# Rotating 96 images by 180 degrees on one core: one load queue in place of two, the third group loaded in two parts, and the order of the turning work

## The chip, the core and the metric

The kernel runs on one core of one Trainium2 chip. The metric is the device time of one execution in microseconds (us). Before the change its median is 121.94 us over three runs, which lie between 121.81 and 122.52 us.

## The reference

```python
def setup_inputs():
    batch, c, h, w = 32, 3, 256, 256
    return {"x": np.random.randn(batch, c, h, w).astype(np.float32)}

def reference(x):
    return np.rot90(x, k=2, axes=(-2, -1)).astype(np.float32)
```

There are 32 x 3 = 96 images of 256 x 256 float32. A turn by 180 degrees reverses both axes, so each image, seen as one run of 65,536 numbers, is written backwards. Nothing is computed; 25.17 MB are read and 25.17 MB are written.

## The kernel before, in words

Each image is cut into four quarters of E = 16384 numbers (64 KB). The 384 quarters make three groups of 128, and each group fills one tile in the on-chip memory SBUF: A, Bt and Ct, with one quarter in each of the 128 partitions. A fourth tile T has J = 2048 columns and is the scratch of the swaps. The quarters of A and Bt are taken alternately from the first 256 quarters, and Ct holds the last 128.

The reversal is done in two steps. Inside a quarter, `swap` (lines 56 to 60) exchanges `w` columns at the left with `w` columns at the right, both reversed, with three VectorE copies through T; line 47 is the copy itself, and it keeps the copies in the order in which they are written. `turn` (line 69) does this from column `lo` to column `hi` of the left half in steps of at most J, so a full turn of a tile is four swaps, or twelve copies of 128x2048. The order of the four quarters of an image is reversed by the store's addresses (line 53, the `::-1`).

Two queues issue transfers: SyncE's (called SPq in the profile, hardware queue q1) and ScalarE's (ACTq, hardware queue q10). Both feed the same 16 DMA engines. SyncE issues the load of A (line 64), then the load of Ct (line 67), and all stores. ScalarE issues the load of Bt (line 66); a memset of 256 columns of Bt on VectorE (line 65) stands ahead of it, so that ScalarE's load waits for it. Each load is one transfer of 128 rows of 64 KB.

The order written out by hand is: turn A except its innermost 2048 columns on either side of the middle; store the first LEAD = 256 columns of A (line 77), a small transfer of 128 pieces of 1 KB; turn Bt up to MID = 2560; turn the rest of A and store the remaining 16128 columns of A (line 80); turn the rest of Bt and store Bt (line 82); turn Ct and store Ct (line 84). A DMA instruction on SyncE holds up the ones written behind it until its own waits are over. A store reads its tile only when the copies that wrote the stored columns are done.

Of the kernel before, what the change touches and what calls it, by code (L numbers as in the profile page):

```python
# [2 lines left out]

os.environ.setdefault("NEURON_RT_ULTRASERVER_MODE", "4")

# [4 lines left out]


@with_exitstack
def kernel(
    ctx: ExitStack,
    tc: tile.TileContext,
    x: bass.AP,
    out: bass.AP,
):
    nc = tc.nc  # L20
    P = 128

    B, C, H, W = x.shape
    L = H * W
    G = 32
    E = L // 4
    J = E // 8

    xr = x.rearrange("b c h w -> (b c) (h w)").rearrange(
        "m (s e) -> (m s) e", s=4)  # L30
    om = out.rearrange("b c h w -> (b c) (h w)").rearrange(
        "m (s e) -> m s e", s=4)
    rows = 2 * P
    x4 = [xr[0:rows:2], xr[1:rows:2], xr[rows:rows + P]]
    o4 = [om[0:2 * G, 1::2], om[0:2 * G, 0::2], om[2 * G:3 * G]]

    pool = ctx.enter_context(tc.tile_pool(name="slots", bufs=1))
    A = pool.tile([P, E], x.dtype, tag="A")
    Bt = pool.tile([P, E], x.dtype, tag="B")
    Ct = pool.tile([P, E], x.dtype, tag="C")  # L40
    T = pool.tile([P, J], x.dtype, tag="T")

    def back(t, lo, hi):
        return t[:, hi - 1:(lo - 1 if lo else None):-1]

    def copy(dst, src):
        tc.keep_in_program_order(nc.vector.tensor_copy(out=dst, in_=src))  # L47

    def load(t, g, lo, hi, queue=nc.sync):
        return queue.dma_start(out=t[:, lo:hi], in_=x4[g][:, lo:hi])  # L50

    def store(t, g, lo, hi):
        return nc.sync.dma_start(
            out=o4[g][:, ::-1, lo:hi], in_=t[:, lo:hi])

    def swap(t, lo, w):
        hi = E - lo - w
        copy(T[:, 0:w], back(t, hi, hi + w))
        copy(t[:, hi:hi + w], back(t, lo, lo + w))
        copy(t[:, lo:lo + w], T[:, 0:w])  # L60

    MID = 2560
    LEAD = 256
    load(A, 0, 0, E)
    nc.vector.memset(Bt[:, 0:256], 0.0)  # L65
    load(Bt, 1, 0, E, nc.scalar)
    load(Ct, 2, 0, E)

    def turn(t, lo, hi):
        while lo < hi:  # L70
            w = min(J, hi - lo)
            swap(t, lo, w)
            lo += w

    half = E // 2
    turn(A, 0, half - J)
    store(A, 0, 0, LEAD)
    turn(Bt, 0, MID)
    turn(A, half - J, half)
    store(A, 0, LEAD, E)  # L80
    turn(Bt, MID, half)
    store(Bt, 1, 0, E)
    turn(Ct, 0, half)
    store(Ct, 2, 0, E)


# [1 line left out]
_INS = ['x']  # L88
_OUTS = [((32, 3, 256, 256), 'float32')]


# [23 lines left out]
```

## Time and profile before

| what | value |
|---|---|
| median of three runs | 121.94 us (121.81 to 122.52) |
| the profiled execution's own time | 121.9 us |
| its span, from first to last instruction | 120.1 us |
| VectorE busy | 44.9 us, 40 instructions |
| bytes by DMA | 50.33 MB, mean 419 GB/s over the span |
| DMA packets' time, share of 16 engines' span | q1 81.3%, q10 16.1% |
| first packet starts, last packet ends (packet records) | 1.74 us, 118.99 us |

A span begins with the core's first instruction; the remaining 1.8 us of the device time lie around it. Times inside the span are counted from its start. In a row of the timeline, the first number is when an instruction starts and the second how long it takes. A DMA issue is short on its queue; its landing is told as the time from the issue until the transfer's completion signal, and that time contains whatever the DMA engines still had to do ahead of it. The trace also records every packet that a DMA engine moved, with its size, start and duration; a load of 128 rows has 128 packets of 65,536 bytes.

### The profile page before, as it was taken

Reading aid. Unit: us, or ns where it says so; the run is one execution under the profiler, and the core shown is the slowest. Engines: PE = TensorE matmul, PEld = TensorE weight load, DVE = VectorE, ACT = ScalarE, POOL = GpSimd, SP = SyncE. Lnnn points to the kernel's source line nnn. Section 1 sums busy time; section 2 is a strip of 40 time slices with the busy share of each in tenths; the row PEclk is TensorE's granted clock in tenths of the full one; section 3 lists DMA queues with packets and bytes.
Section 4 is the critical chain, followed back from the end, with each engine's and each line's share of the span. In section 5 each row is a group of like instructions: output and inputs, shape, how many; then the busy total and the mean of one; then the engine's idle time right before and its main releaser. Section 6 shows DMA issues by size and latency. Waiting matters only on the chain.

```text
span 120.1 us, 97 instructions
## 1 busy us (share of the span) xinstructions
DVE 44.9 (37%) x40; POOL 0.2 (0%) x4
## 2 busy tenths in 40 slices
DVE  0000000000000899999999999999400000000000
POOL 0000000000000000000000000000000000000000
DMA  9888988898889988998899777988898889888980
GB/s 349 349 349 371 677 349 349 349 698 349 349 349 633 415 349 349 546 502 349 349 387 687 344 344 344 687 349 349 349 698 349 349 349 698 349 349 349 677 371 0
DMA packets 1008, 50.33 MB, mean 419 GB/s; under 512 B 112, under 2 KB 240, under 8 KB 240
## 3 DMA queue, kind: packets, MB, share of 16 engines
q1 hardware_dynamic: 864, 41.94, 81.3%
q10 hardware_dynamic: 144, 8.39, 16.1%
HBM read 25.17 MB, written 25.17 MB: 419 GB/s over the span
## 4 chain that ended last, share of the span: by engine, by line
DVE 38%; DMA 32%; issue 1%
DMA A<-in_x_dram 32%; DVE T L47 13%; DVE Bt L47 9%; DVE A L47 8%; DVE Ct L47 8%
## 5 line engine op out<-in xcount | busy, mean ns | idle before, releaser
L47 DVE COPY T<-A 128x2048 f32<-128x2048 f32 x4 | 4.9, 1226 | 38.4 <-DMA A<-in_x_dram 38.3
L47 DVE COPY T<-Bt 128x2048 f32<-128x2048 f32 (+2 forms) x5 | 5.1, 1014 | 0.2
L47 DVE COPY Bt<-T 128x2048 f32<-128x2048 f32 (+2 forms) x5 | 5.1, 1014 | 0.2
L47 DVE COPY Bt<-Bt 128x2048 f32<-128x2048 f32 (+2 forms) x5 | 5.1, 1013 | 0.2
L47 DVE COPY T<-Ct 128x2048 f32<-128x2048 f32 x4 | 4.9, 1227 | 0.1
L47 DVE COPY Ct<-T 128x2048 f32<-128x2048 f32 x4 | 4.9, 1227 | 0.1
L47 DVE COPY A<-T 128x2048 f32<-128x2048 f32 x4 | 4.9, 1227 | 0.1
L47 DVE COPY A<-A 128x2048 f32<-128x2048 f32 x4 | 4.9, 1227 | 0.1
L47 DVE COPY Ct<-Ct 128x2048 f32<-128x2048 f32 x4 | 4.9, 1226 | 0.1
L65 DVE MEMSET Bt<- 128x256 f32 x1 | 0.3, 272 | 0.9 <-PEq L99 0.9
L99 POOL MEMSET const-bfloat16-1.0<- 128x1 bf16 x1 | 0.1, 102 | 0.0
L99 POOL MEMSET const-uint8-127<- 128x1 uint8 x1 | 0.1, 102 | 0.0
L99 POOL MEMSET const-float32-0.0<- 128x1 f32 x1 | 0.1, 99 | 0.2 <-issue 0.2
L99 POOL MEMSET const-float32-1.0<- 128x1 f32 x1 | 0.1, 99 | 0.0
## 6 DMA issues: line engine op xcount, KB each, us to landing
out_dram<-A SPq DMA_DIRECT2D x1, 8064.0 KB, 20.9
out_dram<-A SPq DMA_DIRECT2D x1, 128.0 KB, 18.4
A<-in_x_dram SPq DMA_DIRECT2D x1, 38.7
Bt<-in_x_dram ACTq DMA_DIRECT2D x1, 43.1
Ct<-in_x_dram SPq DMA_DIRECT2D x1, 60.1
out_dram<-Bt SPq DMA_DIRECT2D x1, 29.6
out_dram<-Ct SPq DMA_DIRECT2D x1, 33.9
```

The lines of the kernel that those rows point to most:

```text
L47: tc.keep_in_program_order(nc.vector.tensor_copy(out=dst, in_=src))
L65: nc.vector.memset(Bt[:, 0:256], 0.0)
L99: nc = _bacc.Bacc("TRN2", target_bir_lowering=False, num_devices=1)
```

## The change

All four loads are now issued by SyncE, one behind the other: A, then Bt, then Ct as two transfers, rows 0 to 111 and rows 112 to 127. The memset goes, and ScalarE issues nothing. The pieces of the turning work change: A is turned except its innermost KEY = 128 columns on either side of the middle; the first 256 columns of A are stored as before; Bt is turned up to half - LATE = 6144 columns in place of 2560; then a new copy of 112 partitions by 8 columns from Ct into T stands in the order, which reads rows that the first of the two Ct transfers writes, and whose result nothing uses; then the 128 key columns of A are turned, and A's second store is issued. The rest of Bt (2048 columns), its store, the turn of Ct and its store follow as before. In the changed kernel the lines of `swap` and of the helpers are the same, and the two Ct loads are lines 68 and 69.

```diff
-    MID = 2560
+    R = P - 16
     LEAD = 256
+    LATE = 2048
+    KEY = 128
     load(A, 0, 0, E)
-    nc.vector.memset(Bt[:, 0:256], 0.0)
-    load(Bt, 1, 0, E, nc.scalar)
-    load(Ct, 2, 0, E)
+    load(Bt, 1, 0, E)
+    nc.sync.dma_start(out=Ct[0:R, :], in_=x4[2][0:R, :])
+    nc.sync.dma_start(out=Ct[R:P, :], in_=x4[2][R:P, :])
...
-    turn(A, 0, half - J)
+    turn(A, 0, half - KEY)
     store(A, 0, 0, LEAD)
-    turn(Bt, 0, MID)
-    turn(A, half - J, half)
+    turn(Bt, 0, half - LATE)
+    copy(T[0:R, 0:8], back(Ct, 0, 8)[0:R])
+    turn(A, half - KEY, half)
     store(A, 0, LEAD, E)
-    turn(Bt, MID, half)
+    turn(Bt, half - LATE, half)
     store(Bt, 1, 0, E)
     turn(Ct, 0, half)
     store(Ct, 2, 0, E)
```

## The prediction

> **What bounds the kernel now.** I read the DMA parts of the page first, because the kernel only moves data.
>
> ```profile
> DMA  9888988898889988998899777988898889888980
> DMA packets 1008, 50.33 MB, mean 419 GB/s; under 512 B 112, under 2 KB 240, under 8 KB 240
> ...
> q1 hardware_dynamic: 864, 41.94, 81.3%
> q10 hardware_dynamic: 144, 8.39, 16.1%
> ```
>
> The 16 DMA engines are busy in every slice but the last. The two shares add to 97.4%. 50.33 MB over 16 engines are 48 rows of 64 KB for each, so one row costs at most 0.974 x 120.1 / 48 = 2.44 us. The packet records agree: after the first row of each engine, all 352 load rows up to 59 us took 2.418 to 2.429 us, and the store rows of Bt and Ct 2.418 to 2.441. So a core's floor here is 48 x 2.42 = 116.2 us, and the packets run from 1.74 to 118.99 us, 117.2 us. About 1 us is not floor: the first rows are slow (median 3.11 us, 0.69 over), and some engines idle up to 0.4 us between loads and stores.
>
> The chain looks different, and has to be read with the issues beside it:
>
> ```profile
> DVE 38%; DMA 32%; issue 1%
> ...
> out_dram<-A SPq DMA_DIRECT2D x1, 8064.0 KB, 20.9
> out_dram<-A SPq DMA_DIRECT2D x1, 128.0 KB, 18.4
> A<-in_x_dram SPq DMA_DIRECT2D x1, 38.7
> Bt<-in_x_dram ACTq DMA_DIRECT2D x1, 43.1
> Ct<-in_x_dram SPq DMA_DIRECT2D x1, 60.1
> out_dram<-Bt SPq DMA_DIRECT2D x1, 29.6
> out_dram<-Ct SPq DMA_DIRECT2D x1, 33.9
> ```
>
> It walks back from the last store through VectorE, but that store was issued at 85.4 us and took 33.9 us to land, although 8 rows per engine need 19.4: it queued behind two others for 14 us. VectorE is early there and does not bound. Now the place where the order does matter, the change from loads to stores:
>
> ```profile
> 58.51 1.23 DVE L47 COPY A<-T 128x2048 f32<-128x2048 f32 x1
> 59.76 0.55 SPq L53 DMA_DIRECT2D out_dram<-A  x1
> ...
> 70.31 0.54 SPq L53 DMA_DIRECT2D out_dram<-Bt  x1
> ```
>
> A's large store is issued at 59.76 and its first packets start at 60.97 to 61.20; the engines end their last load rows at 60.32 to 60.85 and fill the gap with the 1 KB pieces. The later stores are issued 10 us and more before their turn.
>
> **The change, part by part.**
>
> *One queue in place of two.* SyncE issues four loads in a row; an issue took 0.38 to 0.43 us, so the last leaves at about 2.4 us, 39 us before an engine needs it. What goes is the sharing of rows between q1 and q10. A then lands after 8 rows: 1.95 (mean first start) + 0.69 + 8 x 2.42 = 22.0 in place of 39.45, Bt at 41.4 in place of 44.3. The DMA engines do the same rows at the same 2.42 us, so this is worth nothing by itself. Its bounds: 0.69 us of gain, if the slow first rows come from the second queue's issue, and 0.3 us of loss. I take 0.
>
> *VectorE.* The memset (0.27) goes. Copies of 512, 1536 and 2048 columns took 427, 960 and 1227 ns, about 160 ns plus 0.52 ns a column; so the recut swaps cost 3 x 1.23 in place of 3 x (0.43 + 0.96) for Bt, and 3 x (1.16 + 0.23) in place of 3 x 1.23 for A: +0.48 - 0.48. The 8-column copy costs 0.16. All lies under the transfers: A is turned by 22.0 + 12 x 1.25 = 37.0, Bt's first three swaps run from 41.4 to 52.8, and then VectorE waits.
>
> *The added wait.* The copy from Ct waits for all 112 rows. Behind it on VectorE stand A's key swap, the rest of Bt and Ct; behind those on SyncE A's large store, then all others. The store is ready 0.18 + 3 x 0.25 = 0.93 us after the 112 rows, and its packets come 1.2 us after that, 2.1 us in all. If the last 16 rows took one row's time, 2.42 us, that and the 1 KB pieces (0.4 us) just cover it: 0 to +0.3 us. If the 16 rows take longer it is hidden wholly. Bt's store would be issued 3 x 1.25 = 3.8 us after A's, needed 19 us after it; Ct's 15 us after the last 16 rows land, needed 39 us after. Nothing there.
>
> *The third group as 112 rows and 16.* This decides. In the trace every transfer touches all 128 partitions, eight rows for each engine, and the rows keep their 2.42 us to 0.5% whatever the other engines do; so the limit is a private path of 64 KB in 2.42 us, 27.1 GB/s, for each share of eight rows, 16 paths in all. The trace does not say whether that path sits in the DMA engine or at the partitions it writes. Sixteen neighbouring rows are the case that separates them. Lower bound: each engine takes one row on a path of its own, 2.42 us. Upper bound: the 16 rows are two shares of eight, on two paths, 8 x 2.42 = 19.4 us. Between lie depths of two (4.84) and four (9.68). I take four: the nearest row is the store of Ct, whose output address is made of 32 runs of four neighbouring partitions, and it goes out at full speed, so runs of four can be the unit dealt to a path; 16 neighbours are then four runs on four paths. So this transfer costs 9.68 in place of the 2.42 that those rows had in the whole load: +7.26. For the 112 rows the depth is seven if the engines are the limit (16.9 us), eight wherever a path keeps all its eight rows (19.4 us): 0 to +2.42. An engine that is through with its seven starts on its sixteenth early, so the two excesses partly overlap: +7.26 to +9.68 together. I take the middle, +8.5.
>
> [...]
>
> **The sum.** Before: loads end at 41.4 + 19.4 = 60.8 (recorded: 60.85), and stores and completion take the rest. After: 60.8 + 8.5 = 69.3, then the same 24 store rows, since each engine keeps its own rows and the slowest sets the end. Span 120.1 + 8.5 = 128.6; device 121.9 + 8.5 = 130.4. The profiled 121.9 is the median of the three runs, so nothing is to be corrected.
>
> **The rivals.** A difference of about 1% (1.2 us) is what this measurement tells from no change.
>
> *The limit sits in the DMA engines (not slower).* Place: lines 68 and 69. Each engine moves seven rows and then one, each 2.42 us, 8 x 2.42 as before, and the loads end at 60.8. Then A's store decides: 112 rows in at 58.5, its packets at 60.6 to 60.9. It decides as soon as the depth of the 16 rows is one. Time 121.6 to 122.4. For it: one constant duration for loads and stores, whose addresses are cut differently (64 x 2 for A and Bt, 32 x 4 for Ct). Against: all of these span 128 partitions, and a deal without collisions would look the same.
>
> *A shallow collision.* Depth two, 4.84 us, or a depth of four half hidden under the 112 rows: +2 to +6, 124 to 128 us.
>
> *A deep collision.* The upper bound, two paths: +16.9 + 2.4, 141 us. Or the 112 rows themselves are dealt row by row, so that at each of seven steps the engines write 16 neighbours: 7 x 9.68 = 67.7 in place of 16.9, and with the last 16 about 180 us. Against the latter: engines drift apart by up to 1 us already in the first rows (1.74 to 2.72), which loosens a lockstep.
>
> *Faster.* All of the 0.69 us of the first rows and the idle 0.4 us together give 120.8, still within 1%; below that only rows under 2.418 us would help, and no load row is.
>
> **How the numbers follow.** The forecast, depth four, +6 to +10.5 us with the uncertain overlap, has its own range of 127.9 to 132.4 and a chance of 0.55. Shallow: 0.10. Limit in the engines: 0.26. Deep: 0.07. Faster by over 1%: 0.02. So slower by over 1% 0.72, within 1% 0.26. The range has to reach to the engines' case, whose lower end with a little gain at the first rows is 121.4; it goes up to 132.4 and leaves out the deep cases and the faster one, 0.09.
>
> **What would show it.** Right: the rows of Ct's last transfer take about 9.7 us each, the two Ct transfers land about 29 us after Bt in place of 19, A's store packets begin at 69 to 70 us, and the store rows are unchanged. The rows of the 112 transfer should vary, some at 4.8 us. If they are all 2.42 while the 16 rows are slow, the sum is 7.3 and the time 129.2. Wrong: all Ct rows at 2.42 us, and the loads over at 61; or idle DMA engines between 60 and 64 us, which would make the wait on the 112 rows the cause.

## The result and the profile after

The changed kernel takes 142.44 us (median of six runs, 142.31 to 142.92) against 121.98 us before (six runs, 121.81 to 122.52): a ratio of 1.168, 95% interval 1.167 to 1.170. It is 20.5 us slower; the forecast was +8.5 us in a range up to 132.4.

From the page of the changed kernel, the DMA lines of the 40 slices (tenths of busy time, then GB/s) and the queue:

```profile
DMA  8696969799798599999390699999999999999990
GB/s 298 298 597 298 597 298 578 317 466 429 317 578 187 112 298 298 298 298 224 75 299 0 230 432 459 422 459 423 410 410 466 429 448 429 448 410 429 466 392 0
DMA packets 1024, 50.33 MB, mean 358 GB/s; under 512 B 128, under 2 KB 256, under 8 KB 256
...
q1 hardware_dynamic: 1024, 50.33, 97.0%
```

The DMA engines are as busy as before (97.0% of a longer span, 97.4% before), but the mean rate fell from 419 to 358 GB/s. Busy is the time that packets take, not the bytes that they move. From the thirteenth slice to the twenty-third (a slice is 3.5 us) the rate is low. Cut by stages, the columns being the stretch, VectorE's and GpSimd's busy time, the clock, the DMA share and GB/s:

```profile
2.00:41.00 39.00, 14.52 (x12) 0.00 (x0) 1.00 0.96 415
41.00:71.00 30.00, 11.04 (x9) 0.00 (x0) 1.00 1.11 258
71.00:82.00 11.00, 4.55 (x8) 0.00 (x0) 1.00 0.77 177
82.00:140.00 58.00, 14.71 (x12) 0.00 (x0) 1.00 0.95 411
```

A packet is counted in the stretch in which it starts, so a share can pass 1. Before the change, the last 20 us of the loads had this rate:

```profile
41.00:61.00 20.00, 19.41 (x18) 0.00 (x0) 1.00 1.03 444
```

The loads of A and Bt (to 41 us) and the stores (from 82 us) run at full rate, 415 and 411 GB/s. Between them lie the two transfers of the third group, at 258 and 177 GB/s. The packet records show it row by row. They do not name the engine; below, the rows are sorted by their start and taken 16 at a time, one for each engine. All sizes are 64 KB.

```
rows of Ct, changed kernel     took, ns (least / median / most)
first of seven                 4076 / 4291 / 4555
second                         4780 / 4791 / 4876
third                          4647 / 4663 / 4853
fourth                         2861 / 3106 / 4888
fifth                          3405 / 3572 / 4702
sixth                          4204 / 4509 / 4652
seventh                        4606 / 4708 / 5304
the last 16 rows               7847 / 8334 / 8842
every row of A and Bt but the first   2418 to 2427
```

VectorE and the added wait, from the timeline:

```profile
52.29 1.23 DVE L47 COPY Bt<-T 128x2048 f32<-128x2048 f32 x1
74.76 0.17 DVE L47 COPY T<-Ct 112x8 f32<-112x8 f32 x1 [21.25 <-DMA Ct<-in_x_dram]
74.97 0.23 DVE L47 COPY T<-A 128x128 f32<-128x128 f32 x1
...
75.74 0.55 SPq L53 DMA_DIRECT2D out_dram<-A  x1
```

The copy waits 21.25 us for the 112 rows, and A's large store is issued at 75.74 in place of 59.76. That looks like the cause, and the chain supports it at first sight, because it walks back from the last store through VectorE to a load:

```profile
DMA 29%; DVE 22%; another core or an unknown queue 17%; issue 1%; SPq 0%; DVEq 0%
...
out_dram<-A SPq DMA_DIRECT2D x1, 8064.0 KB, 25.4
out_dram<-A SPq DMA_DIRECT2D x1, 128.0 KB, 55.8
Ct<-in_x_dram SPq DMA_DIRECT2D x2, 76.4
A<-in_x_dram SPq DMA_DIRECT2D x1, 21.8
Bt<-in_x_dram SPq DMA_DIRECT2D x1, 40.9
```

But the last load row ends only at 81.25, after that issue, so the store was in the queue in good time. The difference of the spans, 140.5 - 120.1 = 20.4 us, is the difference of the times at which the last load row ends: 81.25 against 60.85. It has three terms: the 112 rows took 30.0 us on the mean engine where 7 x 2.42 = 16.9 were free of trouble (+13.1), the 16 rows 8.34 in place of 2.42 (+5.9), and the slowest engine ended 1.63 us behind the mean in place of 0.23 (+1.4).

### The profile page after: what moved, and what is told of

It reads as the page before. It is cut to its first block, busy times and chain, and to the rows that moved or that the text cites. A ratio compares the mean times of both kernels' runs of the same rounds, so it can differ in the third digit from the quotient of the medians.

```text
span 140.5 us, 99 instructions
## 1 busy us (share of the span) xinstructions
DVE 44.8 (32%) x40; POOL 0.2 (0%) x4
## 2 busy tenths in 40 slices
DMA packets 1024, 50.33 MB, mean 358 GB/s; under 512 B 128, under 2 KB 256, under 8 KB 256
## 3 DMA queue, kind: packets, MB, share of 16 engines
q1 hardware_dynamic: 1024, 50.33, 97.0%
## 4 chain that ended last, share of the span: by engine, by line
DMA 29%; DVE 22%; another core or an unknown queue 17%; issue 1%; SPq 0%; DVEq 0%
DMA Bt<-in_x_dram 29%; DVE T L47 7%; DVE Ct L47 7%; DVE Bt L47 7%; DVE A L47 0%; SPq L50 0%; DVEq L47 0%
## 5 line engine op out<-in xcount | busy, mean ns | idle before, releaser
L47 DVE COPY T<-Ct 128x2048 f32<-128x2048 f32 (+1 forms) x5 | 5.1, 1016 | 23.8 <-DMA Ct<-in_x_dram 23.7
L47 DVE COPY T<-A 128x2048 f32<-128x2048 f32 (+2 forms) x5 | 5.1, 1013 | 22.7 <-DMA A<-in_x_dram 22.6
L47 DVE COPY T<-Bt 128x2048 f32<-128x2048 f32 x4 | 4.9, 1227 | 4.8 <-DMA Bt<-in_x_dram 4.7
L47 DVE COPY A<-A 128x2048 f32<-128x2048 f32 (+2 forms) x5 | 5.1, 1014 | 0.2
L47 DVE COPY A<-T 128x2048 f32<-128x2048 f32 (+2 forms) x5 | 5.1, 1014 | 0.2
L47 DVE COPY Bt<-T 128x2048 f32<-128x2048 f32 x4 | 4.9, 1227 | 0.1
L47 DVE COPY Bt<-Bt 128x2048 f32<-128x2048 f32 x4 | 4.9, 1226 | 0.1
```

## The experiments

The theory after the result, an estimate from rows of 4.1 to 5.3 and 7.8 to 8.8 us where 2.42 was usual: a row goes at 2.42 us only if its engine is alone on the path to the partition it writes; several partitions share a path; and the transfers of 112 and 16 rows make engines meet there. The rivals: the wait, the one queue, the mere number of transfers, or a limit inside the engines.

**Whole group, wait kept.**

```diff
-    nc.sync.dma_start(out=Ct[0:R, :], in_=x4[2][0:R, :])
-    nc.sync.dma_start(out=Ct[R:P, :], in_=x4[2][R:P, :])
+    load(Ct, 2, 0, E)
```

> The changed kernel with the third group loaded as one transfer of 128 rows; the copy from Ct then waits for all of it. Theory of colliding rows (the part loads write some partitions over a path that two or four engines share): all rows at 2.42 us, loads over at 61 us; the wait for the whole group costs the 2.1 us from landing to the first packets of A's large store, less the 0.4 us of 1 KB pieces: 123.4 to 124.0 us. Rival, that the one queue or the wait itself costs the 20 us: 140 to 142.4 us.

124.68 us, ratio 1.023 (1.020 to 1.026). Of the 20.5 us 2.7 are left, although the one queue, the order of turning and the copy from Ct stay. Its timeline:

```profile
61.66 0.17 DVE L47 COPY T<-Ct 112x8 f32<-112x8 f32 x1 [8.07 <-DMA Ct<-in_x_dram]
...
62.64 0.55 SPq L53 DMA_DIRECT2D out_dram<-A  x1
```

Here the wait is uncovered: the last load row ends at 61.28 (60.85 before), A's large store is issued at 62.64, its first packets come at 63.84 (60.97 before). These 2.9 us are the difference of the profiled spans, 123.0 against 120.1, so the wait accounts for the 2.7 us of the medians. They are 0.7 more than the upper end expected: the copy starts only 0.38 us after the last load row has ended, and the loads end 0.4 us later than before.

**Only the split, in the kernel before.** The edit is the change's two transfers in place of line 67, and nothing else.

> The kernel before, with nothing changed but the third group's load, which becomes the two transfers of 112 and 16 rows. Colliding rows: the 20 us come back, 140 to 143 us, with rows of 4 to 5 us in the first part and of about 8 us in the second; a little less if the rows of Bt, taken in turn from the other queue, loosen the collisions. Rival (one queue, or the wait): 121.5 to 122.5 us.

142.47 us, ratio 1.167 (1.165 to 1.169): the whole loss, with two queues and without the copy. A's large store is issued as early as before the change (59.76):

```profile
59.81 0.54 SPq L53 DMA_DIRECT2D out_dram<-A  x1
```

The slow rows have the changed kernel's pattern: 4.1 to 4.9 us in five of the seven steps (three rows of the last took 5.0 to 5.9), mostly 2.7 to 3.8 in the fourth and fifth, and 7.2 to 8.8 for the last 16 rows.

**The same bytes split by columns.**

```diff
+    CUT = E - J
+    load(Ct, 2, 0, CUT)
+    load(Ct, 2, CUT, E)
```

in place of the two row transfers.

> The changed kernel with the third group split by columns, 14336 and then 2048 of all 128 partitions, in place of by rows. The bytes ahead of the signal are the same seven eighths, the number of transfers and the wait are the same. Colliding rows: nothing collides, loads over at 61 us, A's large store comes as the loads end: 121.6 to 122.4 us. Rival, that any second transfer for the group or the wait costs: 130 us or more.

122.15 us, ratio 1.002 (1.001 to 1.003). Two transfers and a signal after seven eighths of the bytes, both on all 128 partitions, cost 0.15 us here. A's store packets begin at 61.15, 0.2 us after the loads' end at 60.95:

```profile
58.97 0.17 DVE L47 COPY T<-Ct 112x8 f32<-112x8 f32 x1 [5.62 <-DMA Ct<-in_x_dram]
...
59.95 0.55 SPq L53 DMA_DIRECT2D out_dram<-A  x1
```

**Without the copy from Ct.** Line 81 of the changed kernel goes; the row split stays.

> The changed kernel without the 112x8 copy, so that A's key columns are turned and A's large store is issued at about 54 us, 22 us earlier; the row split stays. Colliding rows: the store still queues behind the slow rows, 142.0 to 142.5 us, as with the wait. Rival, that the wait costs: the 20 us shrink by most of the 22 us.

142.89 us, ratio 1.171 (1.169 to 1.173). A's large store is issued 21 us earlier, and nothing is gained:

```profile
54.40 0.55 SPq L53 DMA_DIRECT2D out_dram<-A  x1
```

These four settle that the split by rows is the cause, and that the 21 us of waiting on VectorE were its effect.

**The ground for the next runs: the store early.** The third group is whole, the copy is gone, and `turn(A, half - KEY, half)` and A's large store stand right behind the first store. Bt is then turned in one go.

> All loads from SyncE, the third group whole, no copy from Ct, and A's large store issued as soon as A is turned (about 38 us), so that it queues behind the loads. This is the ground for the runs that split the third group otherwise. Colliding rows: rows at 2.42 us throughout and no idle engine between loads and stores, 121.4 to 122.2 us. Rival, that an early store disturbs the loads: 123 us or more.

122.81 us, ratio 1.006 (1.004 to 1.008), above the first expectation and just under the rival's. The loads' last row of each engine took 3.3 to 3.8 us; more on this at the end. On this ground the third group's load is cut in other ways.

**112 rows as seven transfers of every seventh partition.**

```diff
-    load(Ct, 2, 0, E)
+    for r in range(7):
+        nc.sync.dma_start(out=Ct[r:112:7, :], in_=x4[2][r:112:7, :])
+    nc.sync.dma_start(out=Ct[112:P, :], in_=x4[2][112:P, :])
```

> As the run with the early store, but the 112 rows come as seven transfers of 16 rows, every seventh partition (0, 7, 14 ... 105, then 1, 8 ... and so on), and rows 112 to 127 as an eighth. If the transfer of 112 rows gives each DMA engine seven neighbouring rows, this is the same sequence of partitions at the engines: rows of 3 to 4.9 us in the same pattern, 29 to 31 us for the seven, 141.5 to 143.5 us in all. If the transfer of 112 rows is dealt out otherwise, or a transfer of 112 rows is slow for its count, the time is another: 132 us or less, or over 150.

142.5 us in one run. The medians of the seven steps are 4.35, 4.73, 4.79, 2.90, 3.56, 4.63 and 4.71 us, against 4.29, 4.79, 4.66, 3.11, 3.57, 4.51 and 4.71 for the transfer of 112 rows. The medians differ by at most 0.21 us; the reading is that the one transfer gives each engine seven neighbouring rows, and that at each step the engines write partitions seven apart. The fourth step shows what may be a single collision: two engines took 4.73 and 4.74 (4.86 and 4.89 in the changed kernel), about twice 2.42, and the others 2.7 to 3.2. In the fifth, two took 4.24 and 4.43 and the others 3.6 to 3.7.

**Sixteen rows at a time, two ways.** The same eight transfers of 16 rows, to every eighth partition or to neighbours:

```diff
+    for r in range(8):                    # every eighth partition
+        nc.sync.dma_start(out=Ct[r:P:8, :], in_=x4[2][r:P:8, :])
```
```diff
+    for r in range(0, P, 16):             # neighbours
+        nc.sync.dma_start(out=Ct[r:r + 16, :], in_=x4[2][r:r + 16, :])
```

> The third group as eight transfers of 16 rows, each to every eighth partition. [...] If a path serves eight neighbouring partitions, or if the limit is in the DMA engines, no two rows meet: 122 us.

> The third group as eight transfers of 16 rows, each to 16 neighbouring partitions; the same number and size of transfers as with every eighth partition. Paths of four neighbours: four rows meet on each of four paths, 9.68 us a row, 77.4 us for the group in place of 19.4, 180 us in all. Paths of eight neighbours: 19.4 us a row, 155 us, 257 us in all. Limit in the DMA engines, or a cost for each transfer alone: the same time as with every eighth partition.

One run each: 143.63 and 176.98 us. From the stages of the run with every eighth partition, then of the run with neighbours:

```profile
41.00:82.00 41.00, 14.72 (x12) 0.00 (x0) 1.00 1.01 211
82.00:140.00 58.00, 14.72 (x12) 0.00 (x0) 1.00 0.99 429
```
```profile
41.00:116.00 75.00, 14.72 (x12) 0.00 (x0) 1.00 1.01 125
116.00:174.00 58.00, 14.72 (x12) 0.00 (x0) 1.00 0.96 416
```

The load stage has 211 and 125 GB/s with full DMA engines (share 1.01), and the stores behind it full rate again (429 and 416). The rows took 5.11 us (median of 128) and 9.22 us: 2.1 and 3.8 times 2.42. The bytes and the number of transfers are the same; what differs is which rows, and so which partitions, go together. So the limit is not in the engines. The reading, an estimate from the factors 2.1 and 3.8, is that two engines meet on a path with every eighth partition, and four with 16 neighbours. By it a path of eight neighbouring partitions is ruled out, as it would have left every eighth partition free of collisions.

One rival stands untested: row and partition go together in all these loads, so the rows that are read at one time lie differently in DRAM too, and no run moves the one without the other. That the partitions decide is the author's estimate and was not shown.

The run with every eighth partition says one thing more. Its sequence is what a load of 128 rows would be if it gave each engine eight neighbouring rows. Whole loads take 2.42 us a row and not 5.11, so by this reading they are dealt to the engines in another way than the 112 rows; how, no trace here shows.

**Two halves of 64 rows.** `range(0, P, 64)` with transfers of 64 neighbouring rows.

> As the run with the early store, but the third group comes as two transfers of 64 neighbouring rows. [...] If two large transfers of equal size are free of collisions: 123 us.

143.0 us in one run, against the 123 us expected of two transfers free of collisions; the rows took 5.12 us (median; 5.11 with every eighth partition), and the group about 40 us. Two large equal parts are no better.

**A store in two parts.** All loads are whole; A's large store goes out as 48 images' rows (96 partitions) and 16 (32 partitions).

```diff
-    store(A, 0, LEAD, E)
+    for m in (slice(0, 48), slice(48, 64)):
+        nc.sync.dma_start(out=o4[0][m, ::-1, LEAD:E],
+                          in_=A[2 * m.start:2 * m.stop, LEAD:E])
```

> As the run with the early store, all loads whole, but A's large store goes out as two transfers, of 96 partitions and of 32. [...] If only writes into the partitions collide: 122.5 to 123.2 us.

141.39 us in one run, far above the 122.5 to 123.2 us expected if only writes into the partitions collide: cut by partitions, a store is slowed as well. Its stages:

```profile
41.00:61.00 20.00, 14.72 (x12) 0.00 (x0) 1.00 1.00 419
61.00:95.00 34.00, 14.72 (x12) 0.00 (x0) 1.00 1.05 332
95.00:138.00 43.00, 0.00 (x0) 0.00 (x0) 1.00 0.75 323
```

The loads keep 419 GB/s; with the store in two parts the rate falls, and the DMA share of the last stretch is only 0.75, because the engines come apart: they start their last rows between 126.3 and 136.0 us. Unlike in the loads, many engines kept their pace: in each of the first two groups of 16 store rows ten took 2.38 us and six 3.0 to 5.4, and in all of the first six groups the median is at most 2.50, while the slowest row took 3.3 to 5.4. Four of the last 16 took 8.5 to 10.0 us; why was not tried.

**The column split with an earlier signal.** `CUT = E - J - 1024`, otherwise as above.

> The run with the split by columns, with the first part 13312 columns in place of 14336, so that the signal comes about 1.2 us earlier and A's large store is in the queue about 1 us before the loads end. If waiting store packets cost nothing and only the gap between loads and stores counts: 121.8 to 122.1 us, at or below the kernel before. If a queued large store slows the last load row, as in the run with the early store: 122.4 to 123.0 us.

122.40 us, ratio 1.002 (1.001 to 1.003), like the split after 14336 columns. The median is at the lower end of the second expectation. The profiled execution, however, took 122.09 us, the shortest of the eleven, so its trace does not show what the median has more. In it A's store packets start at 61.02, and the store rows take 2.38 us from the first one, where the first 16 took 2.38 to 2.42 before, yet the span is the 120.3 us of the other column split. The last load pieces take their 0.46 us; some in work when the store is issued (58.76) took up to 0.73. This run does not tell the two apart. None of the kernels tried is faster than the kernel before.

## Why the prediction was wrong

- **What bounds the kernel:** right. The difference in time is the difference in the end of the load rows, and the stores keep 2.38 to 2.44 us a row. (The load rows behind each engine's first number 368, not 352; all took 2.418 to 2.429 us.)
- **One queue, VectorE, the added wait at no cost:** right in the changed kernel. The column split puts all three together at 0.15 us, though a gain of one could hide in a loss of another. The price of an uncovered wait, put at 2.1 us less 0.4, was 2.7.
- **The split decides, with collisions at the partitions:** right that the split decides: the run with the split alone has the whole loss. That the collisions are at the partitions was not shown: the rows in DRAM are left as the rival.
- **The 16 rows at depth four, 9.68 us:** right in kind. In the run with neighbours, where such transfers follow each other, a row took 9.22 us, 3.8 times 2.42. In the changed kernel it was 8.34; there the engines start these rows over 2.7 us (70.36 to 73.01), which may be why. The term was +7.26 and is +5.9. That the depth came out as four was in part luck: its ground, the runs of four partitions in a store's address, was tested by no run.
- **The 112 rows at 0 to +2.42 us: the step that failed.** It measured +13.1 us. I counted how many of the 112 rows fall to each path in all, at most eight, and took that as the time, as if the paths were kept evenly busy. What counts here is which rows are in work at the same moment: the same eight transfers of 16 rows took 5.11 or 9.22 us a row by that alone. In the seven steps of the 112 rows, no step kept 2.42 us. In the fourth and the fifth, two rows stand out (4.86 and 4.89, 4.51 and 4.70 us), but the other fourteen took 2.9 to 3.3 and 3.4 to 3.6; in the other five steps all 16 took 4.1 to 5.3. So more than two rows of a step are slowed: of the 34.6 us of engine time by which the rows of the fourth and fifth steps exceed 2.42 us each, 25.3 fall to the fourteen others. How many rows meet at a step no trace shows, and why the other rows slow down was not found.
- **The two excesses overlap partly:** wrong in sign. The engines came apart, and the slowest sets the end: +1.4 us in place of up to -2.4.
- **The rivals:** the limit in the engines is refuted by 5.11 against 9.22 us for the same transfers. The deep case of 141 us was near in time but for another reason, a depth of eight for the last 16 rows, which did not occur (they took 8.34 us, not 19.4).

## What to carry to other kernels

Where transfers already run at the floor, here 2.42 us a row, try the cut along the columns, with every part on all 128 partitions, before a cut by rows. Cut into 112 and 16 rows, a load of 19 us took about 20 us longer; the same seven eighths cut along the columns cost 0.2. Look at what the 16 engines touch at the same moment, not at totals for each path: the same 128 rows, 16 at a time, took 5.11 or 9.22 us each by which of them went together. A DMA share near 1 with fewer GB/s than elsewhere in the same kernel (1.11 with 258 GB/s, where the loads of A and Bt had 0.96 with 415) was here the sign of slow packets, 4.1 to 5.3 us for most rows, and the long wait on VectorE (21.25 us) was only its shadow.

## What was not expected of the hardware

- **Where two rows were slow, the whole step was.** In the fourth of the seven steps two engines were slow (4.86 and 4.89 us) and the other fourteen took 2.9 to 3.3 us, none 2.42; in the five steps other than the fourth and fifth all 16 took 4.1 to 5.3. In the first steps of a store in two parts ten of 16 stayed at 2.38. Why loads are coupled and stores less so was not tried and stays open.
- **Sixteen rows at a time took about two or about four times as long as in a whole load:** 5.11 us with every eighth partition and 9.22 with neighbours, against 2.42.
- **With large stores queued early, the last load rows took longer.** With A's store issued 22 us before the loads end, the last load row of an engine took 3.3 to 3.8 us in place of 2.42, and the kernel 122.81 us. With the store issued at 59.76 (before) the last rows stay at 2.42 to 2.43. Bt's store was early in that run too (57.03), so which of the two does it, and at what lead it begins, was not found.
